# Weights of the last batches in one piece or in parts, and the order of their matmuls, in a batched fp32 matmul on one Trainium2 core

## Chip, cores and metric

One core of a Trainium2 chip. The metric is device time in microseconds (us) from start to end. Of before there are runs on several chips; all times below are medians.

## The reference

```python
def setup_inputs():
    batch, m, k, n = 32, 512, 1024, 768
    return {
        "x": np.random.randn(batch, m, k).astype(np.float32),
        "weight": np.random.randn(batch, k, n).astype(np.float32),
    }

def reference(x, weight):
    return np.matmul(x, weight).astype(np.float32)
```

Each of the 32 batches has its own weight, so no weight is used twice: 67.1 MB of x and 100.7 MB of weights are read, and 50.3 MB of output written.

## The kernel before

x and the weights are cast to bf16 by the DMA that loads them, issued by POOL (only batch 0's x comes uncast, from the SP queue). PE transposes x, DVE copies the transposed tiles, PE multiplies into PSUM, and ACT and DVE copy the results out. The outputs up to batch 27 are stored from POOL's queue; those of 28 to 31 from the SP queue, which begins with the first half of batch 30 as soon as that has been copied out, then takes 28, 29, the second half of 30 and both halves of 31. A "half" is the output of one pair of row tiles.

`CHUNKED` names the batches whose weight comes in several DMAs. Their matmuls run through all four row tiles with one part of the weight (so many of the 8 slices of k), then through all four with the next. All four row tiles are therefore finished only near the end of the batch. A batch not named there has its weight loaded at once and its row tiles run one after the other.

```python
    CHUNKED = {B - 4: (4, 4), B - 3: (4, 4), B - 2: (4, 4), B - 1: (4, 2, 2)}
    ...
    w_pool = ctx.enter_context(tc.tile_pool(name="w", bufs=4))
    out_pool = ctx.enter_context(tc.tile_pool(name="out", bufs=3))
    ...
    def load_w(b):
        ws[b] = w_pool.tile([P, KT, N], BF16, name="w_sb")
        at = 0
        for n in CHUNKED.get(b, (KT,)):
            nc.gpsimd.dma_start(out=ws[b][:, at:at + n, :], in_=w_view[b, :, at:at + n, :])
            at += n
    ...
    def evacuate(b, pair, pm):
        o = outs[b][:, pair * N2:(pair + 1) * N2]
        nc.scalar.copy(o[:, 0:512], pm[0])
        nc.vector.tensor_copy(o[:, 512:1024], pm[1])
        nc.scalar.copy(o[:, 1024:N2], pm[2])
    ...
            if b + AHEAD < B:              # AHEAD = 3
                load_w(b + AHEAD)
            if b == B - LATE:              # LATE = 4: the last two stores of POOL
                store(b // 2 - 2)
                store(b // 2 - 1)
            if b == B - 1:                 # the stores of batches 28 to 30
                halves = [slice(pair * N2, (pair + 1) * N2) for pair in range(2)]
                nc.sync.dma_start(out_view[b - 1, :, halves[0]], outs[b - 1][:, halves[0]])
                for late in range(B - LATE, B - 2):
                    nc.sync.dma_start(out_view[late], outs[late])
                nc.sync.dma_start(out_view[b - 1, :, halves[1]], outs[b - 1][:, halves[1]])
    ...
            pms = [banks() for _ in range(2)]
            at = 0
            for n in CHUNKED[b]:
                last = at + n == KT
                for mt in range(MT):
                    matmuls(pms[mt // 2], mt % 2, xT[mt], b, range(at, at + n), True)
                    if last and mt % 2 == 1:
                        pair = mt // 2
                        evacuate(b, pair, pms[pair])
                        if b == B - 1:
                            nc.sync.dma_start(out_view[b, :, halves[pair]], outs[b][:, halves[pair]])
                at += n
```

## Time and profile before

| | before |
|---|---|
| time, median of 3 runs | 514.59 us (514.52 to 514.7) |
| span of the profiled core | 512.7 us |
| moved to and from HBM | 218.1 MB, 425 GB/s over the span |
| end of the last copy (ACT) | 502.44 us |
| second half of batch 31 handed to the SP queue | by 502.79 us |

The prediction shows the lines these come from and reads them.

### The profile page before, as it was taken

What the parts mean: (1) busy time and instruction counts of PE and PEld (TensorE: products, weight loads), DVE (VectorE), ACT (ScalarE), POOL (GpSimd) and SP (SyncE); (2) the same over time, 40 slices, a digit from 0 to 9 for tenths busy, and PEclk for the clock granted to TensorE, in tenths of its full rate; (3) what the DMA queues carried; (4) which work ended last, traced back from release to release, by engine and by line L of the source; (5) the groups of instructions that cost most, each with busy time, mean ns of one, the idle gap of its engine ahead of it and who ended that gap; (6) DMA issues with size and microseconds to landing.
All of it is one profiled execution on the core that took longest, in us unless ns stands there. A gap on an engine that the chain in (4) does not pass through costs nothing.

```text
span 512.7 us, 5785 instructions
## 1 busy us (share of the span) xinstructions
PE 435.4 (85%) x2576; PEld 278.7 (54%) x2576; DVE 130.0 (25%) x196; ACT 76.1 (15%) x129; POOL 39.1 (8%) x73
## 2 busy tenths in 40 slices
PE   1806999999999996997989989798898989999991
PEld 1504666666666663654646546464464645666660
DVE  0202324141515141320413205041040410514121
ACT  1100121212121201111111111111101111120201
POOL 3000010101010101001010000101001000010000
PEclk9956999999999998997999989899798998999997
DMA  8999999999999999999999999999999999999998
GB/s 240 224 221 213 218 220 216 333 221 310 243 218 336 215 324 231 228 325 220 330 223 234 318 223 334 217 247 304 221 333 218 258 295 220 331 215 212 320 427 345
DMA packets 12712, 135.63 MB, mean 265 GB/s; under 512 B 1296, under 2 KB 1296, under 8 KB 3088
## 3 DMA queue, kind: packets, MB, share of 16 engines
q0 software_dynamic: 11440, 126.88, 96.6%
q1 hardware_dynamic: 1248, 8.39, 4.1%
q8 instruction: 20, 0.33, 0.2%
q14 instruction: 4, 0.03, 0.0%
HBM read 167.77 MB, written 50.33 MB: 425 GB/s over the span
## 4 chain that ended last, share of the span: by engine, by line
PE 46%; DMA 37%; issue 8%; DVE 5%; another core or an unknown queue 1%; POOL 1%; ACT 0%; SPq 0%; POOLq 0%
PE pm L123 40%; DMA w_sb<-in_weight_dram 28%; DMA one_sb<-in_x_dram 8%; PE pt L78 5%; DVE xT L85 4%; DVE out_sb L144 1%; POOL out_dram L164 0%; PE pt L105 0%; POOL w_sb L70 0%; POOL x_sb L60 0%; DVE one_sb L144 0%; DVE xT L93 0%; ACT out_sb L145 0%; SPq L151 0%
## 5 line engine op out<-in xcount | busy, mean ns | idle before, releaser
L123 PE MATMUL pm<-w_sb,xT 128*128 128x256 bf16 (+1 forms) x2048 | 353.7, 336 | 26.4 <-DMA w_sb<-in_weight_dram 26.2
L123 PEld LDWEIGHTS <-xT 128*128 128x128 bf16 x2048 | 205.3, 101 | 170.3 <-DMA w_sb<-in_weight_dram 29.3
L144 DVE COPY out_sb<-pm 128x512 f32<-128x512 f32 x62 | 42.9, 691 | 317.6 <-PE pm L123 317.6
L78 PE MATMUL pt<-ident,x_sb 128*128 128x128 f32 x496 | 79.8, 302 | 10.5 <-DVE xT L85 10.2
L78 PEld LDWEIGHTS pt<-ident,x_sb 128*128 128x128 f32 x496 | 69.3, 209 | 21.5 <-DVE xT L85 18.7
L85 DVE COPY xT<-pt 128x1024 bf16<-128x1024 bf16 x120 | 77.4, 687 | 11.0 <-PE pt L78 11.0
L143 ACT COPY out_sb<-pm 128x512 f32<-128x512 f32 x62 | 36.3, 585 | 271.7 <-PE pm L123 271.7
L145 ACT COPY out_sb<-pm 128x512 f32<-128x512 f32 x62 | 36.3, 585 | 145.7 <-PE pm L123 145.6
L70 POOL DMA_DIRECT2D w_sb<-in_weight_dram x37 | 20.1, 544 | 404.8 <-PE pm L123 397.6
L105 PE MATMUL pt<-ident,one_sb 128*128 128x128 f32 x8 | 1.9, 421 | 19.1 <-DMA one_sb<-in_x_dram 19.1
L106 DVE CAST xT<-pt 128x512 bf16<-128x512 f32 x8 | 5.8, 733 | 34.6 <-PE pt L105 34.1
L105 PE MATMUL pt<-ident,x_sb 128*128 128x128 f32 x24 | 5.3, 383 | 10.5 <-DMA x_sb<-in_x_dram 10.3
L105 PEld LDWEIGHTS pt<-ident,one_sb 128*128 128x128 f32 x8 | 1.6, 219 | 19.4 <-issue 19.4
L164 POOL DMA_DIRECT2D out_dram<-out_sb x14 | 10.1, 719 | 6.7 <-ACT out_sb L143 3.5
L105 PEld LDWEIGHTS pt<-ident,x_sb 128*128 128x128 f32 x24 | 4.1, 209 | 11.5 <-issue 10.3
L60 POOL DMA_DIRECT2D x_sb<-in_x_dram x15 | 8.1, 539 | 10.9 <-DMA w_sb<-in_weight_dram 10.9
L144 DVE COPY one_sb<-pm 128x512 f32<-128x512 f32 x2 | 1.4, 690 | 9.0 <-PE pm L123 9.0
L93 DVE COPY xT<-pt 128x1024 bf16<-128x1024 bf16 x4 | 2.6, 686 | 0.2 <-PE pt L78 0.2
L143 ACT COPY one_sb<-pm 128x512 f32<-128x512 f32 x2 | 1.2, 585 | 6.4 <-PE pm L123 6.4
L145 ACT COPY one_sb<-pm 128x512 f32<-128x512 f32 x2 | 1.2, 585 | 1.6 <-PE pm L123 1.6
L143 ACT ACT_TABLE_LOAD x1 | 1.3, 1283 | 0.7 <-PEq L232 0.7
L64 POOL DMA_DIRECT2D x_sb<-in_x_dram x1 | 0.5, 528 | 2.1 <-DMA w_sb<-in_weight_dram 2.1
(6 smaller groups left out, 0.9 us busy)
## 6 DMA issues: line engine op xcount, KB each, us to landing
w_sb<-in_weight_dram POOLq DMA_DIRECT2D x28, 1536.0 KB, 41.7
out_dram<-out_sb POOLq DMA_DIRECT2D x14, 3072.0 KB, 55.3
x_sb<-in_x_dram POOLq DMA_DIRECT2D x15, 2048.0 KB, 49.8
w_sb<-in_weight_dram POOLq DMA_DIRECT2D x7, 768.0 KB, 38.2
out_dram<-out_sb SPq DMA_DIRECT2D x2, 1536.0 KB
x_sb<-in_x_dram SPq DMA_DIRECT2D x1, 1536.0 KB
out_dram<-one_sb SPq DMA_DIRECT2D x2, 768.0 KB
out_dram<-out_sb SPq DMA_DIRECT2D x2, 768.0 KB
```

The source lines that it names most:

```text
L60: nc.gpsimd.dma_start(out=xs[b], in_=pair_view[b // 2])
L70: nc.gpsimd.dma_start(out=ws[b][:, at:at + n, :], in_=w_view[b, :, at:at + n, :])
L78: nc.tensor.transpose(pt[:, j, :], pairs[:, mo, j::JT], ident)
L85: nc.vector.tensor_copy(both[:, :, :, :, half, :].rearrange("p b j i r -> p j b i r"), words(b, mt + MT * half).rearrange("p j (b i r) -> ...
L93: nc.vector.tensor_copy(xT.rearrange("p j m r -> p (j m r)"), words(B - 1, mt).rearrange("p j m -> p (j m)"))
L105: nc.tensor.transpose(pt[:, i, :], rows[:, JT * h + i::KT], ident)
L106: nc.vector.tensor_copy(xT[:, 2 * h:2 * h + 2].rearrange("p j m r -> p j r m"), pt.rearrange("p (j r) m -> p j r m", r=2),)
L123: nc.tensor.matmul(pm[bank][:, at:at + size], xT[:, ko // 2, :, ko % 2], ws[b][:, ko, off:off + size], start=(ko == 0 and not (together an ...
L143: nc.scalar.copy(o[:, 0:512], pm[0])
L144: nc.vector.tensor_copy(o[:, 512:1024], pm[1])
L145: nc.scalar.copy(o[:, 1024:N2], pm[2])
L164: nc.gpsimd.dma_start(out=two_view[at], in_=twos[at])
```

## The change

Its intent: parts let PE begin a batch before its weight is whole, at the price of more DMA issues and of late copies. Only batch 28 keeps them. In 29, 30 and 31 the weight comes whole, and the first pair of row tiles can be copied out, and for 31 stored, at half time.

```diff
-    CHUNKED = {B - 4: (4, 4), B - 3: (4, 4), B - 2: (4, 4), B - 1: (4, 2, 2)}
+    CHUNKED = {B - 4: (4, 4)}
...
+            if b in CHUNKED:
+                pms = [banks() for _ in range(2)]
+                at = 0
+                for n in CHUNKED[b]:
+                    for mt in range(MT):
+                        matmuls(pms[mt // 2], mt % 2, xT[mt], b, range(at, at + n), True)
+                        if at + n == KT and mt % 2 == 1:
+                            evacuate(b, mt // 2, pms[mt // 2])
+                    at += n
                 continue
...
+            for pair in range(2):
+                pm = banks()
+                for half in range(2):
+                    mt = 2 * pair + half
+                    if mt not in xT:
+                        xT[mt] = transpose_first(mt)
+                    matmuls(pm, half, xT[mt], b, range(KT), False)
+                evacuate(b, pair, pm)
+                if b == B - 1:
+                    nc.sync.dma_start(out_view[b, :, halves[pair]], outs[b][:, halves[pair]])
```

(The removed lines are the chunked loop shown above and the same row-tile loop at its old place.)

More of the change, by code (lines that the diff above doesn't have):

```diff
@@ L195 @@
                 xT = {mt: ready.pop((b, mt)) for mt in range(MT)}
-            if b not in CHUNKED:
-                for pair in range(2):
-                    pm = banks()
-                    for half in range(2):
-                        mt = 2 * pair + half
-                        if mt not in xT:
-                            xT[mt] = transpose_first(mt)
-                        matmuls(pm, half, xT[mt], b, range(KT), False)
-                    evacuate(b, pair, pm)
-                continue
-            pms = [banks() for _ in range(2)]
-            at = 0
-            for n in CHUNKED[b]:
-                last = at + n == KT
-                for mt in range(MT):
-                    matmuls(pms[mt // 2], mt % 2, xT[mt], b, range(at, at + n), True)
-                    if last and mt % 2 == 1:
-                        pair = mt // 2
-                        evacuate(b, pair, pms[pair])
-                        if b == B - 1:
-                            nc.sync.dma_start(out_view[b, :, halves[pair]], outs[b][:, halves[pair]])
-                at += n
+            if b in CHUNKED:
[7 more added lines that the diff above has]
+                    at += n
+                continue
+            for pair in range(2):
[8 more added lines that the diff above has]
+                    nc.sync.dma_start(out_view[b, :, halves[pair]], outs[b][:, halves[pair]])
 _INS = ['x', 'weight']
```

## The prediction

> **What bounds the kernel now.** I read the page's span and slices first, to see which engine is full.
>
> ```profile
> span 512.7 us, 5785 instructions
> PE   1806999999999996997989989798898989999991
> DMA  8999999999999999999999999999999999999998
> HBM read 167.77 MB, written 50.33 MB: 425 GB/s over the span
> ```
>
> The DMA row is 9 from the second slice to the last but one. The kernel moves 167.77 + 50.33 = 218.10 MB, and 218.10 MB over 512.7 us is the 425 GB/s shown. So transfers bound it over the whole span. PE looks nearly full too (85% busy), so the second question is which of the two sets the last 60 us, where the change lies. For that I read the chain of work that ended last, its last part:
>
> ```profile
> 373.89 49.68 DMA w_sb<-in_weight_dram
> 423.57 0.05 issue
> 423.62 12.05 PE pm L123 x63
> ...
> 441.54 20.60 PE pm L123 x127
> ...
> 468.01 20.60 PE pm L123 x127
> ...
> 491.41 10.41 PE pm L123 x64
> 501.82 0.02 issue
> 501.85 0.59 ACT out_sb L145
> ```
>
> From 423.6 us this chain has no DMA piece: PE goes from batch to batch with only the 6 us of transposes between pairs. It ends at 502.44 us though, and the span is 512.7 us, so 10 us follow that no engine works in. The table of stretches tells what they are (columns: length, busy us of PE, PE loads, DVE, ACT and POOL with counts, then granted clock, DMA share, GB/s; a weight is cast from fp32 to bf16 on its way, so some 215 GB/s written is some 430 read):
>
> ```profile
> 468.00:478.00 10.00, 10.00 (x64) 6.03 (x62) 1.43 (x3) 1.75 (x3) 0.00 (x0) 1.00 1.03 211
> 491.00:497.00 6.00, 6.00 (x40) 3.68 (x39) 1.14 (x2) 0.00 (x0) 0.00 (x0) 1.00 1.01 425
> 497.00:502.00 5.00, 4.81 (x30) 2.73 (x28) 1.06 (x2) 1.86 (x4) 0.00 (x0) 1.00 1.02 433
> 502.00:506.00 4.00, 0.00 (x0) 0.00 (x0) 0.32 (x1) 0.43 (x1) 0.00 (x0) 0.95 0.98 415
> 506.00:510.00 4.00, 0.00 (x0) 0.00 (x0) 0.00 (x0) 0.00 (x0) 0.00 (x0) 0.50 0.95 396
> 510.00:512.70 2.70, 0.00 (x0) 0.00 (x0) 0.00 (x0) 0.00 (x0) 0.00 (x0) 0.50 0.19 77
> ```
>
> The DMA share stays at 0.95 or more until 510 us, 8 us after PE has stopped: stores queued earlier are still draining. Last, the timeline of the SP queue and of ACT, to see when the last stores were handed over:
>
> ```profile
> 486.86 0.39 SPq L182 DMA_DIRECT2D out_dram<-one_sb  x1
> 487.30 2.31 SPq L184 DMA_DIRECT2D out_dram<-out_sb  x2
> 489.72 1.11 SPq L185 DMA_DIRECT2D out_dram<-one_sb  x1
> 501.16 1.63 SPq L216 DMA_DIRECT2D out_dram<-out_sb  x2
> ```
>
> The last line is the two halves of batch 31, 768 KB (0.786 MB) each. The second is handed over by 502.8 us. At 425 GB/s it needs 1.9 us, yet the end is 10 us later: it stands behind others.
>
> **What the Trainium skill says.**
> 1. "HBM Reference", section Specifications: a core that streams alone reaches about 425 GB/s, bounded by its 16 DMA engines. The trace agrees, with 425 GB/s over the span. No order of transfers can then save much; only fewer bytes or a filled gap could.
> 2. "DMA: Bandwidth & Descriptors", section Queues, rings and completion order: each DMA engine takes turns between its queues, a packet at a time. The trace agrees: in 494 to 496 us the POOL queue moved 47 packets (0.55 MB) and the SP queue 52 (0.31 MB, in smaller packets). So stores of the SP queue that start earlier take turns from the POOL queue; bytes change places, none vanish.
> 3. The same page, its table of measured loads under Bandwidth: 341 GB/s for a 1 MB load, 425 for a 16 MB one; it advises batching. That would favour whole weights. The trace shows no such loss here, because the queue is never empty: written GB/s were 218 in 470 to 474 us (pieces of 768 KB) and 207 in 474 to 478, where smaller ones begin, with a DMA share of 1.04 and 1.01.
> 4. "TensorE: Matmul & The Clock Gate", section Back-to-back issue gap: a warm gap is N/2.4 + 2.5 ns. For 32 matmuls of 512 and 32 of 256 columns that makes an estimate of 32 x (215.8 + 109.2) = 10.4 us a batch, in either order; the page also has a lower rate for sustained streams, which the trace doesn't show. Its 10.41 us for the 64 matmuls of batch 31, chunked, and its 20.60 us for batches 27 (row tile by row tile) and 28 (chunked) together, agree with 10.4. The order of the matmuls costs nothing at full clock.
>
> **The change part by part.**
> Loads. Batch 29: two DMAs become one; 30: two become one; 31: three become one. That removes 4 POOL issues of about 0.53 us, or 2.1 us of an engine that is 8% busy: nothing on the path. The bytes, and their order in the POOL queue, stay: weights 28, 29, the last x, weights 30, 31, two stores of 3.1 MB. Each POOL transfer waits for the one eight places before it: the last x went out at 423.86 us when weight 26 had landed. With four fewer transfers these waits fall away. The order of issue with its waits shows x then waiting for a store of long before, weight 30 for weight 26, and the two stores for loads landed by 441 us. So x should be issued at about 421.3, weight 31 at 452.2 (it needs the buffer of batch 27, as now), the stores at about 452.8 and 453.5 instead of 459.49 and 463.14. They only join a full queue earlier.
>
> Arrival. A whole weight can't be used before its last part has landed. Its last part lands when it does now:
> - 29: I take 463.0, since the second store's issue at 463.14 waited for its second half. PE needs it at 467.85: 4.8 us to spare.
> - 30: second half issued 440.81 + 34.2 = 475.0 us. PE needs it at 478.2 (467.85 + 10.3): 3.2 us.
> - 31: third part issued 455.48 + 26.9 = 482.4. PE needs it at 491.25: 8.9 us.
> Batch 28 stays in parts; it is the one that lands as PE wants it (404.7 + 46.7 = 451.4 against 451.7). So PE should not wait: cost 0.
>
> Matmuls. 3 x 64, same sizes, same count of weight loads: 0 us. PE ends at 501.8 again.
>
> Evacuation. Chunked, a batch's first pair of row tiles was ready only near its end; now it is ready at half time. From batch 27, already whole: copies at 2.7, 5.2, 5.4 us and 7.9, 10.4, 10.6 us after its first matmul. For batch 30 (from 478.2) the first half is copied out by about 484.1 instead of 486.7, so the SP stores begin at 484.2, 2.7 us earlier. For batch 31 (from 491.25) the first half is out at about 497.3 and is issued then instead of at 501.16: 3.9 us earlier. The second half finishes with the last matmul, as before: 501.85 + 0.59 = 502.44.
>
> The end. What remains to be moved at 502.4 us, by the stretches: 0.98 x 3.6 + 0.95 x 4 + 0.19 x 2.7 = 7.8 us of all engines. The last half, 0.786 MB, is 1.9 us of it, so 5.9 us of other stores lie before it. Bytes moved up to then are equal in both kernels, as DMA is full in both, so the same 7.8 us remain and the end is the same. What can change is the tail: from 506 us the DMA engines leave 0.05 x 4 + 0.81 x 2.7 = 2.4 us unfilled, and I take about 2 us of that as unavoidable completion and uneven finish. I grant 0.2 us to earlier stores.
> Sum: 514.59 + 0 (loads) + 0 (PE) - 0.2 (tail) = 514.4 us.
>
> **The rivals.**
> A. A wait for a whole weight takes the place of the wait for parts. Against it: the margins above. Even a 3 us delay of PE would be absorbed in part by the 5.9 us that lie before the last half, less some 3 us that a store takes from issue to its first packet (the SP stores issued at 486.86 show none before 490). If weight 30 came 5 us later than I think, PE would end 2 us later and the time would be at most 1 to 2 us longer.
> B. The earlier SP stores collide with weight 31 or with the store whose buffer batch 31 reuses. Batch 31's output takes the buffer of batches 24 and 25; that store landed at 459.49 + 30.3 = 489.8. The copy now wants it at 493.9 instead of 499.8. With SP packets flowing from about 487 instead of 490, I expect that landing near 490.5. For the rival: 3.4 us of margin instead of 10. If it fails, only the first half's store slips, by some us out of 5: no change of the end.
> C. The early store fills the tail, or larger transfers run faster. The most a level finish can bring is about 1 us (513.6). A 1% higher rate over the three weights (9.4 MB read, 22 us) would be 0.2 us.
> D. PE is the bound, and freer evacuation speeds it up. Against it: from 423.6 us PE waits for nothing but its transposes, and these follow the last matmul of the batch before in both kernels. Worth 0.
>
> **Range and chances.** The three runs of before lie within 0.2 us. A and C reach 1 to 2 us up and 1 us down; another chip or day may add some tenths. Eight times in ten I expect 513.5 to 515.5. A 2% change is 10.3 us, more than any rival makes: 1.5% faster, 97% within 2%, 1.5% slower.
>
> **What would show it.** Right: the chain again without a DMA piece after 423.6 us; PE's last matmul near 501.8; the stores of POOL issued near 453 us; the SP queue starting near 484 us and the first half of batch 31 near 497; DMA share of 0.95 or more until about 510. Wrong: a wait of PE on w_sb at about 467.9, 478.2 or 491 us; an ACT or DVE wait on a DMA at 494; a DMA share well under 0.9 somewhere between 485 and 508; or the last half's store landing long after all the others, which would mean that it, and not the sum of the bytes, sets the end.

## The result, and the profile after

| | before | after |
|---|---|---|
| median of 6 runs each, same rounds | 514.64 us | 514.36 us |
| lowest to highest | 514.44 to 515.07 | 514.2 to 514.7 |
| ratio of after to before | | 0.9995, 95% interval 0.9982 to 1.0008 |

A ratio here is always the mean time of one kernel's runs over that of the other's of the same rounds, so not quite the ratio of the medians. The interval holds 1: the same time.

The head of the page of the changed kernel:

```profile
span 512.6 us, 5733 instructions
DMA  8999999999999999999999999999999999999998
HBM read 167.77 MB, written 50.33 MB: 426 GB/s over the span
```

Same bytes, same full row. (The instruction count fell by 52: 4 are the DMA issues saved. The other 48 are matmuls, 2528 on the page instead of 2576, though both programs hold the same matmuls: records missing from the trace, not work saved.)

The POOL and SP timelines show that all that was meant to move did move:

```profile
453.21 0.53 POOL L70 DMA_DIRECT2D w_sb<-in_weight_dram  x1 [15.54 <-PE pm L123]
453.79 1.43 POOL L164 DMA_DIRECT2D out_dram<-out_sb  x2
...
485.23 0.39 SPq L182 DMA_DIRECT2D out_dram<-one_sb  x1
485.68 2.35 SPq L184 DMA_DIRECT2D out_dram<-out_sb  x2
490.43 0.33 SPq L185 DMA_DIRECT2D out_dram<-one_sb  x1
498.23 5.53 SPq L215 DMA_DIRECT2D out_dram<-out_sb  x2
```

POOL's two last stores are issued at 453.8 us at once, instead of at 459.5 and 463.1. The SP queue begins at 485.2 instead of 486.9. The last line stands for both halves of batch 31: the first goes out at 498.2, the second ends the 5.53 us at 503.8.

The end of the chain of waits has no wait for a weight, as before. Its last pieces:

```profile
494.06 8.18 PE pm L123 x50
...
502.30 0.50 PE pm L123 x2
502.80 0.02 issue
502.82 0.59 ACT out_sb L145
```

And the table of stretches at the end (columns as in the prediction; the two last ones are DMA share and GB/s):

```profile
497.00:502.00 5.00, 5.00 (x33) 2.96 (x31) 0.69 (x1) 1.17 (x2) 0.00 (x0) 1.00 1.02 433
502.00:506.00 4.00, 0.73 (x4) 0.27 (x3) 0.69 (x1) 0.59 (x1) 0.00 (x0) 1.00 0.97 412
506.00:510.00 4.00, 0.00 (x0) 0.00 (x0) 0.00 (x0) 0.00 (x0) 0.00 (x0) 0.68 0.93 389
510.00:512.70 2.70, 0.00 (x0) 0.00 (x0) 0.00 (x0) 0.00 (x0) 0.00 (x0) 0.50 0.14 57
```

In this execution PE stood about 1 us later than in the profile of before well ahead of the changed part (batch 27 began at 442.35 us, not 441.38), and its last copy ended at 503.41 instead of 502.44. (In both kernels PE waited for weight 26 until about 423.65 us; then batch 26 took 13.15 us here and 12.25 us before, part of it at half the clock. Run to run such a stretch differs, see the last section.) The span is still 512.6 against 512.7 us. That is a first hint that PE's end does not set the kernel's.

### The profile page after: what moved, and what is told of

The parts are those of the page before. It is cut to its first block, busy times and chain, and to the rows that moved or that the text cites. A ratio compares the mean times of both kernels' runs of the same rounds, so it can differ in the third digit from the quotient of the medians.

```text
span 512.6 us, 5733 instructions
## 1 busy us (share of the span) xinstructions
PE 431.9 (84%) x2528; PEld 278.5 (54%) x2576; DVE 130.0 (25%) x196; ACT 76.2 (15%) x129; POOL 37.0 (7%) x69
## 4 chain that ended last, share of the span: by engine, by line
PE 46%; DMA 37%; issue 8%; DVE 5%; another core or an unknown queue 2%; POOL 1%; ACT 0%; SPq 0%; POOLq 0%
PE pm L123 40%; DMA w_sb<-in_weight_dram 29%; DMA one_sb<-in_x_dram 8%; PE pt L78 5%; DVE xT L85 4%; DVE out_sb L144 1%; PE pt L105 0%; POOL out_dram L164 0%; POOL x_sb L60 0%; POOL w_sb L70 0%; DVE one_sb L144 0%; DVE xT L93 0%; ACT out_sb L145 0%; SPq L151 0%
## 5 line engine op out<-in xcount | busy, mean ns | idle before, releaser
L123 PE MATMUL pm<-w_sb,xT 128*128 128x256 bf16 (+1 forms) x2000 | 349.7, 334 | 31.2 <-DMA w_sb<-in_weight_dram 28.7
L78 PE MATMUL pt<-ident,x_sb 128*128 128x128 f32 x496 | 79.8, 303 | 10.4 <-DVE xT L85 10.1
L70 POOL DMA_DIRECT2D w_sb<-in_weight_dram x33 | 18.0, 546 | 406.4 <-PE pm L123 405.6
```

The costliest lines, as they stand in the source:

```text
L78: nc.tensor.transpose(pt[:, j, :], pairs[:, mo, j::JT], ident)
L123: nc.tensor.matmul(pm[bank][:, at:at + size], xT[:, ko // 2, :, ko % 2], ws[b][:, ko, off:off + size], start=(ko == 0 and not (together an ...
```

## The experiments

The theory: the DMA engines are full to the end, so the end comes when the sum of the bytes has been moved, and PE has some slack. The rivals: PE's end, or the place of the last store in its queue, sets the end; or two effects of opposite sign cancel. Eleven kernels ran, with 5 rounds each; they ran with shared runs of before. All runs fell in the fast state; PE + 10.4 us has four of them (the record doesn't say what became of the fifth), the other ten kernels five.

| kernel | median us | ratio to before, 95% interval |
|---|---|---|
| changed kernel | 514.36 | 0.9995 (0.9982 to 1.0008) |
| order alone | 514.60 | 0.9998 (0.9984 to 1.0012) |
| whole loads alone | 514.46 | 0.9997 (0.9984 to 1.0009) |
| batch 28 whole too | 514.60 | 0.9998 (0.9985 to 1.0010) |
| first half held back | 514.37 | 0.9994 (0.9981 to 1.0007) |
| PE + 2.6 us | 514.47 | 0.9995 (0.9982 to 1.0009) |
| PE + 5.2 us | 514.59 | 1.0001 (0.9988 to 1.0014) |
| PE + 7.8 us | 516.66 | 1.0038 (1.0026 to 1.0051) |
| PE + 10.4 us | 519.13 | 1.0088 (1.0074 to 1.0102) |
| PE - 7.8 us | 514.54 | 0.9997 (0.9985 to 1.0010) |
| 0.786 MB less stored | 512.57 | 0.9958 (0.9945 to 0.9970) |
| batch 31 stored from ACT | 514.75 | 0.9999 (0.9985 to 1.0013) |

The intervals are about 0.0013 wide to each side, 0.7 us: a difference smaller than that, such as the 0.2 or 0.3 us of some expectations, can't be told from none. The changed kernel was not run again. It was run at another time. The median of before was 514.62 to 514.70 us, and 514.64 beside the changed kernel.

### The two halves of the change

Order alone:

```diff
-    CHUNKED = {B - 4: (4, 4)}
+    CHUNKED = {B - 4: (4, 4), B - 3: (4, 4), B - 2: (4, 4), B - 1: (4, 2, 2)}
-            if b in CHUNKED:
+            if b == B - 4:
```

> Half of the change: the weights of batches 29 to 31 still come in parts (2, 2 and 3), only their matmuls run row tile by row tile. Theory (the end is set by the sum of the bytes, PE has some 2 us of slack): 514.4 us, within 0.3 us of both kernels, though the SP stores begin some 2 us earlier and the first half of batch 31 goes out near 497 to 498 us. Rival (earlier stores fill the tail): 0.5 to 1 us faster than before.

Whole loads alone (against before):

```diff
-        for n in CHUNKED.get(b, (KT,)):
+        for n in ((4, 4) if b == B - 4 else (KT,)):
```

> The other half: the weights of 29 to 31 come whole, their matmuls still run in parts across all four row tiles. Theory: within 0.3 us of before, POOL's two last stores issued near 453.5 us instead of 459.5 and 463.1, SP stores as late as before. Rival (bigger transfers run faster): 0.3 us or more faster.

Measured: 514.60 and 514.46 us, neither to be told from before. Each half did its own work in the trace: with the order alone, POOL's stores were issued at 459.8 and 463.5 as before, but the SP queue began at 484.6; with the loads alone, POOL's stores went out at 452.8, but the SP queue began at 486.9. So two effects of opposite sign that cancel are not there, unless they are smaller than the 0.7 us that these runs resolve. Nor do whole loads run faster: the writing of weights in 470 to 474 and 474 to 478 us went at 210 and 215 GB/s with the loads alone made whole, at 207 and 218 in the changed kernel, and at 218 and 207 in parts.

### One step further: batch 28 whole as well

```diff
-    CHUNKED = {B - 4: (4, 4)}
+    CHUNKED = {}
```

> The change carried one step on: the weight of batch 28 whole as well, row tile by row tile. It lands at about 455 us while PE wants it at 452.7 or before, so PE should wait 2.5 to 3.5 us at its start and end at about 505.5 to 506.5 us. Theory: the slack of PE (some 2.3 us: from the hand-over of the last half at 503.8 us, 3.4 us to its first packet, 1.9 us to move it, 1.5 us to the end make 510.6, against 512.6) takes up most of it; 0 to 1.5 us slower than the changed kernel, 514.4 to 515.9. Rival (PE is on the path, any wait counts in full): 2.5 to 3.5 us slower.

Measured: 514.60 us; the changed kernel's nearest kin on the same chip in the same rounds (the one with the first half held back) had 514.37. That is inside the band expected, and not resolved from 0. But PE lost more than expected: 3.82 us of waiting, and more after it. Its timeline and the table of stretches (the clock is the third number from the end) show what happened:

```profile
455.75 13.18 PE L123 MATMUL pm<-w_sb,xT 128*128 128x512 bf16 x63 [3.82 <-DMA w_sb<-in_weight_dram]
...
455.75:460.00 4.25, 4.25 (x14) 1.95 (x15) 0.00 (x0) 0.00 (x0) 0.00 (x0) 0.50 1.02 216
460.00:465.00 5.00, 5.00 (x28) 2.97 (x28) 0.69 (x1) 1.17 (x2) 0.00 (x0) 0.89 1.01 211
465.00:468.90 3.90, 3.85 (x26) 2.48 (x25) 0.15 (x1) 0.59 (x1) 0.00 (x0) 1.00 1.06 223
```

After 3.82 us without work the granted clock was 0.50 for over 4 us, and the batch took 13.18 us instead of 10.56. So the last copy ended at 509.03 us, 5.6 us later than in the profile of the changed kernel, where 505.5 to 506.5 had been expected for PE. The profiled execution was the slowest of its five, at 514.98 us; the other four took 514.42 to 514.63. So for batch 28 the parts do what they were made for: without them PE waits. Yet keeping them buys nothing that these runs can measure.

### The early store given away

```diff
-                if b == B - 1:
-                    nc.sync.dma_start(out_view[b, :, halves[pair]], outs[b][:, halves[pair]])
+                if b == B - 1 and pair == 1:
+                    for p in (1, 0):
+                        nc.sync.dma_start(out_view[b, :, halves[p]], outs[b][:, halves[p]])
```

> The changed kernel, but the store of batch 31's first half is issued after that of its second half, so the 3 us won by the earlier evacuation are given away. Theory: at 503.8 us the queue still holds over 4 us of other stores, so nothing is left idle: 514.4 us, within 0.3. Rival (the earlier first half shortens the end): 0.5 us or more slower than the changed kernel.

Measured: 514.37 us against 514.36. Both halves were issued at 502.5 us. The earlier hand-over, the one thing in the change that looked like a gain, is worth nothing that shows here; the 0.5 us of the rival is below what the intervals resolve, but the two medians give no sign of it.

### How much slack PE has

Dead matmuls ahead of batch 31's, overwritten by the pass that counts (n = 1, 2, 3, 4; 2.6 us each):

```diff
+                    if b == B - 1 and pair == 0 and half == 0:
+                        for _ in range(n):
+                            matmuls(pm, half, xT[mt], b, range(KT), False)
                     matmuls(pm, half, xT[mt], b, range(KT), False)
```

> The changed kernel with 16 dead matmuls (one row tile's pass repeated, 2.6 us) ahead of batch 31's. Right result. Theory: PE's slack of some 2.3 us takes up nearly all: 0 to 0.7 us slower than the changed kernel. Rival (PE on the path): 2.6 us slower.

> The same with 64 dead matmuls, 10.4 us. Theory: slack used up, the rest counts in full: 10.4 - 2.3 = 8.1 us slower than the changed kernel, 522.5 us, with a stretch of idle DMA before the last half. Rival PE on the path: 10.4 us slower. Rival no bound by PE at all within this reach: 0.

These two came out at 514.47 and 519.13 us: 0.1 and 4.8 us over the changed kernel, where 0 to 0.7 and 8.1 had been expected. The first fits both what I expected and more slack than that; the second is a miss. 10.4 us of PE cost only 4.8, so the slack was some 5.6 us, not 2.3. Two more runs were made to test that number:

> 32 dead matmuls (5.2 us) ahead of batch 31's. The two runs before showed 0.1 us for 2.6 us and 4.8 us for 10.4 us, so a slack of about 5.6 us rather than 2.3. If so: 0 to 0.4 us slower than the changed kernel. Rival (the old 2.3 us, with the rest spread out): 1.5 to 2.9 us slower.

> 48 dead matmuls (7.8 us). A slack of 5.6 us gives 2.2 us slower than the changed kernel, 516.6 us; a straight line through the two earlier runs from 2.6 to 10.4 us would give 3.2 us.

They came out at 514.59 and 516.66 us: 0.2 and 2.3 us over the changed kernel. So there is a corner between 5.2 and 7.8 us, and the two slower kernels agree on it: 10.4 - 4.8 = 5.6 and 7.8 - 2.3 = 5.5, each good to about 0.7 us.

Why 2.3 was wrong shows in the run with 10.4 us. Its stretches, its last copy and its SP timeline:

```profile
506.00:510.00 4.00, 4.00 (x27) 2.37 (x25) 0.69 (x1) 0.85 (x2) 0.00 (x0) 1.00 0.51 210
510.00:514.00 4.00, 2.40 (x15) 1.24 (x13) 0.69 (x1) 0.90 (x2) 0.00 (x0) 1.00 0.18 72
...
512.44 0.59 ACT L145 COPY out_sb<-pm 128x512 f32<-128x512 f32 x1 [2.12 <-PE pm L123]
...
507.85 5.53 SPq L218 DMA_DIRECT2D out_dram<-out_sb  x2
```

Now the queue does run dry: the DMA share falls to 0.51 and 0.18 while PE works. The last copy ended at 513.03 us and the span is 517.2: a half stored alone needs 4.2 us from the copy's end to the end of the kernel. I had reckoned 6.8, with 3.4 us until the first packet, taken from the SP stores issued at 486.9 whose first packets showed only around 490. Those were issued while POOL's transfers kept the DMA engines full. Here the engines were empty: the last half was issued at 513.05 us and its first packets show between 513.8 and 513.9, 0.8 us later. The slack of PE is what remains when these 4.2 us are taken from the end: with the last copy at 502.5, as in most profiles, 512.6 - 502.5 - 4.2 = 5.9 us, near the 5.5 to 5.6 measured. The same figure gives the span of the other profiles that end late: with batch 28 whole 509.03 + 4.2 = 513.2 us, just past the corner; with 7.8 us of dead work 510.31 + 4.2 = 514.5; with 5.2 us 508.38 + 4.2 = 512.6, at the corner itself. Each is the span of that profile.

### Less PE, fewer bytes

Both give wrong results on purpose.

```diff
# PE - 7.8 us: 48 of the 64 matmuls of batch 31 left out
-                    matmuls(pm, half, xT[mt], b, range(KT), False)
+                    matmuls(pm, half, xT[mt], b, (0, KT - 1) if b == B - 1 else range(KT), False)
# 0.786 MB less: the second half of batch 28 is not stored
-                for late in range(B - LATE, B - 2):
-                    nc.sync.dma_start(out_view[late], outs[late])
+                nc.sync.dma_start(out_view[B - LATE, :, halves[0]], outs[B - LATE][:, halves[0]])
+                nc.sync.dma_start(out_view[B - 3], outs[B - 3])
```

> The changed kernel with 48 of the 64 matmuls of batch 31 left out, 7.8 us of PE (wrong result on purpose). Theory: 0, within 0.3 us of the changed kernel. Rival (PE's end sets the end): up to 7.8 us faster.

> The changed kernel without the store of the second half of batch 28, 0.786 MB less of 218.1 (wrong result on purpose). Theory: at 425 GB/s 1.85 us faster than the changed kernel, 512.5 us, since that is still within PE's slack. Rival (the hand-over of the last half sets the end): 0.

Measured: 514.54 us, so 7.8 us less of PE bring nothing; and 512.57 us, 1.8 us less than the changed kernel, where 0.786 MB at 425 GB/s make 1.85. In the profile with less PE the last copy is done and the last stores are issued 16 us before the end of the span at 512.6 us:

```profile
495.48 0.58 ACT L145 COPY out_sb<-pm 128x512 f32<-128x512 f32 x1 [0.17 <-PE pm L123]
...
494.79 1.78 SPq L215 DMA_DIRECT2D out_dram<-out_sb  x2
```

This pair is the plainest proof: the end follows the bytes and not PE. It leaves one rival: the store left out stood in the SP queue ahead of the last half, so the gain could come from the last half's place in its queue. The next run is for that.

### The last store in a queue of its own

```diff
-                    nc.sync.dma_start(out_view[b, :, halves[pair]], outs[b][:, halves[pair]])
+                    nc.scalar.dma_start(out_view[b, :, halves[pair]], outs[b][:, halves[pair]])
```

> The changed kernel with both halves of batch 31 stored from the ACT queue, so that they take turns with the SP queue's stores instead of standing behind them. Theory (the sum of the bytes sets the end, whoever is last): 514.4 us, within 0.3. Rival (the last half's place in its queue sets the end): 1 us or more faster.

Measured: 514.75 us, the same, where this rival had asked for 1 us or more. Taking turns with the SP queue instead of standing behind it only changes who is last. One thing more is in this trace: the first half of batch 31 was issued on the ACT queue at 498.64 us, with nothing before it there, and its first packets show only between 502.0 and 502.5. So the wait of some 3 us is not one for earlier transfers of the same queue; it is there when the engines are full with another's.

No kernel here with a right result beats before or the changed kernel. The version without any parts (batch 28 whole too) is the simplest, and its time is the same within the interval, but it stands at the corner: any further PE work at the end would cost time there.

## Why the prediction was right or wrong

- Time and range. 514.4 us predicted, 514.36 measured; within 513.5 to 515.5. That they agree to 0.04 us is luck: single runs of the changed kernel lie between 514.2 and 514.7.
- The bound. Right, and shown: bytes taken away bring their full time, PE time taken away nothing.
- Loads and arrival: cost 0. Right. The rule that a POOL transfer waits for the one eight places before it fits the trace of before: x waited for weight 26 (2.10 us), the second part of weight 30 for the x load of 390.49 us (4.11), the third part of weight 31 for the second of weight 28 (2.18). None of these waits is left. The last x was issued at 420.9 us (predicted 421.3), POOL's stores from 453.8 (predicted 452.8 and 453.5). The whole weights landed at 420.40 + 42.1 = 462.5, 437.14 + 38.3 = 475.4 and 453.21 + 28.9 = 482.1 us, each within 0.5 us of the time taken for its last part. From 441 us on PE waited for no weight. The one narrow margin named, batch 28's 0.3 us, did turn into a wait in the run with the first half held back, where PE came 1.5 us earlier to it: 1.41 us, without effect on the time.
- Matmuls: 0. Right in the run with the order alone and in the changed kernel's 10.56 us for batch 31.
- Evacuation. Right in kind: the SP queue began at 485.2 and the first half of 31 went out at 498.2, both 1 us after the predicted times, as PE stood 1 us later in this execution. Rival B did not come: the first copy of batch 31 waited for PE alone.
- The tail: -0.2 us. Not shown. From 506 us the changed kernel left 0.07 x 4 + 0.86 x 2.7 = 2.6 us unfilled, before 2.4; giving the early store away cost nothing. The measured 0.3 us between the medians lies within the interval, and none of the runs ties it to a cause.
- Rival A's size. Wrong: its "some 3 us that a store takes from issue to its first packet" is a wait while the DMA engines are full, not a latency of the store, and was taken off the slack without need. It made no difference to the number predicted, but the two first expectations of slack inherited it. Measured: 4.2 us for the whole of the last half alone, and a slack of 5.5 to 5.6 us.
- Left out of rival A: what a wait does to the clock. Had a weight come late, PE would have lost the wait and more: 2.6 us on top of 3.8 in the run with batch 28 whole. The trace of before had this to show: its batch 26 took 12.25 us after a wait of 3.22, not 10.56.
- Rivals C and D: whole loads were no faster (0.9997, 0.9984 to 1.0009), and freer copies did not speed PE up (10.56 us for batch 31 in both kernels).

What stays open: which of the 2.4 to 2.6 us of unfilled DMA time in the tail could be won. No run addressed it.

## What to carry to other kernels

When the transfers are full to the last microseconds, ask of each change whether it alters the sum of the bytes or leaves a gap; an earlier start, a freer queue or fewer issues only change who is last. Measure the slack of the other engine by adding dead work until the time moves: the corner tells more than a busy share, and the run past it shows the true latency of the last step. Don't take a latency from a transfer that was issued while the DMA engines were full.

## What the Trainium skill lacked or had wrong

- "DMA: Bandwidth & Descriptors", table of measured loads under Bandwidth, and its rule to batch to 1 MiB or more: it doesn't say whether the rates hold for loads one at a time or for a queue of them. With the queue full, weights in two or more parts were written at 218 and 207 GB/s in two stretches of 4 us, whole ones at 210 and 215 (loads alone) or 207 and 218 (changed kernel), and the time was the same (ratio 0.9997).
- The same page, section Queues, rings and completion order: it lacks how long a transfer waits for its first turn when the engines are full with another queue's packets. First packets came 3.4 to 3.6 us after the issue at 486.86 us (SP, beside POOL's) and 3.4 to 3.9 us after that at 498.64 us (ACT, beside SP's), but 0.8 us after the issue at 513.05 us, with the engines empty.
- "TensorE: Matmul & The Clock Gate", section Back-to-back issue gap: it says that the formula N/2.4 + 2.5 over-counts for large N in a stream of loads and matmuls (131 ns for N = 512). Here it did not: 32 matmuls of 512 and 32 of 256 columns, each with its weight load, took 10.4 us, which is the formula's sum. (The prediction calls the 131 ns a "lower rate"; it is a shorter spacing.)
- The same page, section What's actually happening: about 3.4 us of idling bring half the clock. The runs agree only roughly. The clock was 0.50 after waits of 3.82 us (batch 28 whole) and 3.22 us (before, 423.6 us), but shorter waits cost as much: of the 26 waits for a weight between 30 and 470 us in the traces of before, of the changed kernel and of batch 28 whole, each of the 24 of 2.19 to 5.48 us was followed by a batch of 11.87 to 13.38 us instead of 10.56, and the two of 0.23 and 2.10 us by one of 10.57. The clock fell 2.3 us after the last matmul in one place (batch 28 whole, 451.9 to about 454.3 us) and 4.7 us after it in another (end of the changed kernel, 502.8 to about 507.5 us). So what is to be added to a wait when a late load is weighed is 1.3 to 2.8 us here, once the wait is over 2.1 us.
